# The last step of a matrix product takes its seven sub-products in an order that completes one half of the tokens first, and the outputs are multiplied by VectorE alone

## The chip, the cores and the metric

The kernel runs on one core of one Trainium2 chip. A core has TensorE (PE in the profile; PEld is its weight load), VectorE (DVE), ScalarE (ACT), GpSimd (POOL), and SyncE (SP), which here issues the transfers between the chip's memory (HBM) and the on-chip memory SBUF. TensorE writes its results into PSUM, eight banks of 128 partitions x 2 KB. The metric is the device time of one execution in microseconds (us), the median of several runs.

## The reference

One step of a hybrid flow-matching layer over 640 tokens (512 latent, 128 context), each a vector of 2048. What matters here is its end: the channel mixer's down projection, the gated residual, and the final RMSNorm, in float32.

```python
D_MODEL = 2048; D_FF = 5632; RMS_EPS = 1e-6

def _rmsnorm(x, g):
    xf = x.astype(F32)
    y = xf * lax.rsqrt(jnp.mean(xf * xf, axis=-1, keepdims=True) + RMS_EPS)
    return (y * g).astype(x.dtype)

def _layer(x, mod, s0, shift_fn, lp):
    ...
    h = _rmsnorm(x, lp['norm2_g']) * (1.0 + sc2) + sh2
    ff = (jax.nn.silu(h @ lp['w_ffn_gate']) * (h @ lp['w_ffn_up'])) @ lp['w_ffn_down']
    return x + g2 * ff, s_fin

y_prompt = _rmsnorm(x_ctx, final_norm_g)      # 128 tokens
y_sample = _rmsnorm(x_lat, final_norm_g)      # 512 tokens
```

## The kernel before

All 640 tokens stand side by side as columns (T = 640), and the model's 2048 channels as 16 blocks of 128 partitions. Only the last stage is touched by the change: `ff @ w_ffn_down`, and what follows it.

**Seven products instead of eight.** Output channels are made in pairs of blocks (m = 0, 1), tokens in two halves (h = 0: columns 0 to 319, h = 1: columns 320 to 639), the sum over D_FF in two halves. That is a 2x2 by 2x2 block product, and `seven` (L1581) computes it by seven products M1 to M7 of sums of blocks. `PORD` (L1337) is their order: 1, 2, 3, 7, 5, 6, 4. With h first, the outputs are: (0,0) = M1+M2; (1,0) = M1+M6+M5+M3; (0,1) = M1+M6+M7+M4; (1,1) = M1+M6+M7+M5. In the reference's terms two token blocks of 128 (t = 3, 4) lie wholly in h = 1, two (t = 0, 1) in h = 0, and t = 2 lies in both.

**Weights.** Each product's weight block (`rawd`, 128x512) is split by `parts` (L1388) into `hi` (ScalarE) and `lo` (VectorE, `raw - hi`), three buffers of each; each product is then 12 matmuls of 128 x 320 (L1602 to L1604). Sums of weight blocks are made by GpSimd (L1515): `t3` for M7 and the new b12 for M5 before the first product, b22 for M6 and b21 for M4 in place after the third.

**Steps.** A step is one channel pair n in one chunk of the D_FF sum; there are six chunks of eight pairs. In the last chunk n runs from 7 down to 0; each product starts from a sum kept in SBUF (`acc`), which `filled` (L1892) brings into a PSUM bank two products ahead (matmul L1898, ScalarE copy L1899). `Last` (L1831) then joins the seven results of a pair into `cs[0]`, `cs[1]`: VectorE L1851 to L1867, and `out` (L1837, L1840), which multiplies by the gate and adds the residual `xs` (loaded by `load_x1`, L1829, over the buffers of the pair before). The results come to `Last` through a queue `hooks`, three products late (`lag`). `rows` (L1872) turns a finished pair with ten TensorE transposes (L1880), copies it to `acc` as rows of tokens (L1881) and sums squares into `sse` (L1884), both on ScalarE. Through `later`, `out` for h = 1 runs in the third product and `rows` in the fifth product of the following step.

**The end.** After the last pair (n = 0): L1945 to L135 make 1/rms of all five token blocks; then ten output tiles (five token blocks x two halves of the channels, 128x1024, 512 KB each) are multiplied by 1/rms and by `final_norm_g` (which `fg` holds in `acc`), t = 0 to 4 in order. For t = 0, 2, 4 VectorE does both in one instruction (L1957). For t = 1, 3 ScalarE scales (L1954) and GpSimd multiplies (L1955). SP sends each tile (L1958).

The program is ordered per engine by a scheduler from the order of the code and from priorities; each engine then takes its own list strictly in order.

Of the kernel before, what the change touches and what calls it, by code (L numbers as in the profile page):

```python
# [19 lines left out]
P = 128  # L20
D = 2048
KB = D // P
T = 640
NT = T // P
HALF = T // 2
# [11 lines left out]
RMS_EPS = 1e-6  # L37
# [13 lines left out]
CHK = (3, 3, 4, 4, 4, 4)  # L51
# [4 lines left out]
ROWO = 4  # L56
# [31 lines left out]
def flow_step(ctx: ExitStack, tc, x_prompt, x_sample, state_rwkv, c, c_ctx, w_mod, b_mod,  # L88
              norm1_g, w_in, mu_shift, w0, w2, a0, a2, g2, k_k, k_a, r_k, gn_w, gn_b,
              gmlp_ln_g, gmlp_ln_b, w_spatial, b_spatial, w_out, norm2_g, w_ffn_gate,  # L90
              w_ffn_up, w_ffn_down, final_norm_g, y_prompt, y_sample, new_state, dbg=None):
    nc = tc.nc
# [20 lines left out]
    ident = cp.tile([P, P], F32, name="ident")  # L113
# [20 lines left out]
    def rsqrt(out, in_):  # L134
        return G.tensor_tensor(out=out, in0=in_, in1=mhalf.to_broadcast(list(in_.shape)), op=ALU.pow)  # L135
# [1199 lines left out]
    X = {}  # L1335
    t1, t2 = slice(0, HALF), slice(HALF, T)
    PORD = (1, 2, 3, 7, 5, 6, 4)  # L1337

    def xpool(i, j):
        return xep if i < 3 and j < 4 else xcp if j < 4 else xdp  # L1340
# [237 lines left out]

        return pP.tile([P, 512], F32, tag="P", name=f"P{i}")[:, 0:HALF], False

    def seven(b11, b12, b21, b22, x, hook, nk=4, bank=fresh, last=True):  # L1581
# [6 lines left out]
        src = {1: b11, 2: b21, 3: b22, 7: t3, 5: b12, 6: b22, 4: b21}  # L1588
        order = [raw for i in PORD for raw in src[i]]

        ready = [parts(order.pop(0), nk)]
        for o, i in enumerate(PORD):
            ps, filled = bank(i)
            nq = len(b11)
            for q in range(nq):
                hi, lo = ready.pop()
                if order:
                    ready.append(parts(order.pop(0), nk))
                for k in range(nk):
                    xk = x(i, 4 * q + k)  # L1600
                    f, l = q == 0 and k == 0 and not filled, q == nq - 1 and k == nk - 1 and last
                    TE.matmul(ps, hi[:, k, :], xk[:, 0, :], start=f, stop=False)  # L1602
                    TE.matmul(ps, hi[:, k, :], xk[:, 1, :], start=False, stop=False)  # L1603
                    TE.matmul(ps, lo[:, k, :], xk[:, 0, :], start=False, stop=l)  # L1604
# [190 lines left out]

    dn = ctx.enter_context(tc.tile_pool(name="dn", bufs=1))
    acc = dn.tile([P, 8, 7 * HALF], F32, name="acc")
    sse = dn.tile([P, NT, 8], F32, name="sse")
# [32 lines left out]
    class Last:  # L1831
# [11 lines left out]
        def __call__(self, o, p):  # L1843
            n, ps = self.n, self.ps
            ps[PORD[o]] = p
            if o == 1:
                self.xs = xqs.pop(n)
                self.cs = [xap.tile([P, T], F32, tag=next(ctags), name="cd") for _ in range(2)]
                self.tp = tp = xap.tile([P, 2, HALF], F32, tag="rs2", name="tp")
                S.copy(tp[:, 0], ps[1])  # L1850
                V.tensor_add(self.cs[0][:, t1], ps[2], tp[:, 0])  # L1851
                self.out(0, 0)
            elif o == 4:
                act = self.cs[1]
                S.copy(act[:, t2], ps[5])
                V.tensor_add(act[:, t1], ps[3], act[:, t2])
            elif o == 5:
                act, pa, pq = self.cs[1], self.tp[:, 0], self.tp[:, 1]
                V.tensor_add(pq, ps[6], pa)
                V.tensor_add(act[:, t1], act[:, t1], pq)  # L1860
                V.tensor_add(pq, ps[7], pq)
                V.tensor_add(act[:, t2], act[:, t2], pq)
                self.out(1, 0)
            elif o == 6:
                nc.sync.dma_start(acc[:, n, 5 * HALF:5 * HALF + 256],
                                  final_norm_g[n * 256:(n + 1) * 256].partition_broadcast(P))
                V.tensor_add(self.cs[0][:, t2], ps[4], self.tp[:, 1])  # L1867
                later.append((2, lambda: (self.out(1, 1), self.out(0, 1))))
                later.append((ROWO, self.rows))
                load_x1(n - 1)  # L1870

        def rows(self):  # L1872

            n, cs = self.n, self.cs
            for q0 in (0, 2, 4):
# [6 lines left out]
                for t in range(nt):  # L1882
                    junk = dn.tile([P, 256], F32, tag="junk", name="junk2")
                    S.activation(junk, pr[:, t], AF.Square, accum_out=sse[:, q0 + t, n:n + 1])  # L1884

    later = []
    NC = len(CHK)

    fill = [(n, i) for n in range(7, -1, -1) for i in PORD]
    banks = {}  # L1890

    def filled(n, i):  # L1892
# [10 lines left out]
    for s, (c, n) in enumerate(steps):  # L1903
# [12 lines left out]
            bank = fresh  # L1916
        if c >= NC - 2 and (final or turn):
            lag[0] = LAST_LAG
        for o in seven(b11, b12, b21, b22, lambda i, k: XD[i, k], None if turn else Last(n) if final else Sum(n),
                       CHK[c], bank, not turn):  # L1920
            if s % 8 == 6 and c < NC - 1 and o in (2, 3, 4):
                load(c + 1, (1, 2, 7)[o - 2])
            if turn:
                now(turn_ops(c + 1), o)
            elif after and o == 0:
                put_in(6)
                direct(c, 4)
            if o > 2:
                next(dloads, None)
            if final and after and o == 2:  # L1930
                load_x1(n)
            while later and o >= later[0][0]:
                later.pop(0)[1]()
            if s == len(steps) - 1 and o == 5:
                while hooks:
                    hooks.pop(0)()
    while hooks:
        hooks.pop(0)()
    for _, work in later:
# [1 line left out]
    xcx.close()  # L1941
    xex.close()
    fin = ctx.enter_context(tc.tile_pool(name="fin", bufs=5))
    rs = dn.tile([P, NT], F32, name="rse")
    V.tensor_reduce(out=rs, in_=sse, axis=AX.X, op=ALU.add)  # L1945
    V.tensor_scalar(rs, rs, 1.0 / D, RMS_EPS, op0=ALU.mult, op1=ALU.add)
    rsqrt(rs, rs)
    fg = acc[:, :, 5 * HALF:5 * HALF + 256]
    for t in range(NT):
        for h in range(2):  # L1950
            out = fin.tile([P, 4, 256], F32, tag=f"out{h}", name="out")
            src, f = (ap[:, 4 * h:4 * h + 4] for ap in (acc[:, :, t * 256:(t + 1) * 256], fg))
            if t == 1 or t == 3:
                S.activation(out, src, AF.Copy, scale=rs[:, t:t + 1])  # L1954
                G.tensor_tensor(out=out, in0=out, in1=f, op=ALU.mult)  # L1955
            else:
                V.scalar_tensor_tensor(out=out, in0=src, scalar=rs[:, t:t + 1], in1=f, op0=ALU.mult, op1=ALU.mult)  # L1957
            nc.sync.dma_start(yrows(t)[:, h * 1024:h * 1024 + 1024], out.rearrange("p n c -> p (n c)"))  # L1958
    xax.close()

# [28 lines left out]
```

## Time and profile before

| what | us |
|---|---|
| median of 3 runs | 3312.3 (3306.03 to 3312.47) |
| the profiled execution's own time | 3317.92 |
| its span, first to last instruction | 3316.1 |
| last matmul of the last step starts | 3289.72 |
| 1/rms is there, output tiles begin | 3296.05 |
| last output tile is sent | 3311.77 |

Times in the profile are microseconds from the span's start. A row of the timeline gives start, length, engine, line, operation, output <- inputs, shape, and, in brackets, how long the engine stood idle before it and what ended that. A row of the table by stretches gives from:to, the length, the busy time of PE, PEld, DVE, ACT and POOL (with counts), the granted TensorE clock, the share of the 16 DMA engines, and GB/s.

### The profile page before, as it was taken

To read this page: it belongs to the slowest core of one execution; us is meant where nothing else is said; L and a number is where in the kernel's file an instruction comes from. 1 tells how busy PE (TensorE), PEld (TensorE's weight loads), DVE (VectorE), ACT (ScalarE), POOL (GpSimd) and SP (SyncE) were. 2 spreads that over 40 slices of the span, in tenths; PEclk is the share of its full clock that TensorE was granted. 3 is DMA by queue.
4 is the path that set the end of the run, shared out by engine and by line. 5 is a ranking of instruction groups with operands and counts; after the bars stand their busy time and mean duration, and the time that the engine had idled before them with its cause. 6 is when DMAs were issued, how large, how long until landed. Compare 5 with 4: busy or idle time off the path is not lost.

```text
span 3316.1 us, 72388 instructions
## 1 busy us (share of the span) xinstructions
PE 3151.8 (95%) x28216; PEld 2912.2 (88%) x28216; DVE 2409.3 (73%) x4152; ACT 1452.3 (44%) x3163; POOL 1278.7 (39%) x1114
## 2 busy tenths in 40 slices
PE   6899999999999999998999999999999999999996
PEld 3688788778877888888999999999999999999996
DVE  4448767766866677767877777877778787877787
ACT  3334444444443444334644444444444445444365
POOL 0001122222212113333155655656656555555543
PEclk8899999999999999999999999999999999999998
DMA  8767676767667488735534343443443454553453
GB/s 318 247 180 212 184 203 186 184 182 202 187 179 217 129 273 272 237 118 158 166 103 123 118 121 118 120 128 108 125 127 103 129 185 150 162 156 116 139 162 118
DMA packets 740142, 550.88 MB, mean 166 GB/s; under 512 B 140712, under 2 KB 673208, under 8 KB 730968
## 3 DMA queue, kind: packets, MB, share of 16 engines
q1 hardware_dynamic: 727480, 532.57, 53.7%
q0 software_dynamic: 9984, 13.13, 1.7%
q8 instruction: 222, 3.64, 0.5%
q14 instruction: 120, 0.98, 0.1%
q10 hardware_dynamic: 2336, 0.57, 0.1%
HBM read 437.79 MB, written 110.95 MB: 165 GB/s over the span
## 4 chain that ended last, share of the span: by engine, by line
PE 74%; DVE 10%; DMA 6%; issue 5%; POOL 3%; ACT 2%; SPq 0%; DVEq 0%; ACTq 0%; POOLq 0%
PE P L1604 15%; PE P L1603 15%; PE P L1602 15%; PE big L188 4%; PE big L190 4%; PE big L189 4%; PE pG L636 2%; PE pm L881 2%; DMA raw<-in_w_in_dram 2%; DMA wt<-in_w_mod_dram 1%; PE big L1013 1%; DVE lo L1392 1%; PE big L1449 1%; PE big L1447 1%; PE big L1448 1%
## 5 line engine op out<-in xcount | busy, mean ns | idle before, releaser
L1602 PE MATMUL P<-xo,hi 128*128 128x320 f32 x2352 | 728.2, 310 | 3.3 <-ACT hi L1391 3.3
L1604 PE MATMUL P<-xo,lo 128*128 128x320 f32 x2352 | 728.3, 310 | 2.0 <-DVE lo L1392 1.9
L1603 PE MATMUL P<-xo,hi 128*128 128x320 f32 x2352 | 728.1, 310 | 0.0
L1392 DVE TENSOR_TENSOR lo<-raw,hi 128x512 fp32r<-128x512 f32 x532 | 513.7, 969 | 169.1 <-ACT hi L1391 164.5
L1391 ACT CAST hi<-raw 128x512 fp32r<-128x512 f32 x532 | 330.7, 622 | 496.8 <-PE P L1603 389.7
L188 PE MATMUL big<-h_hi,hi 128*128 128x320 f32 x1376 | 452.3, 329 | 8.4 <-ACT hi L166 4.9
L1602 PEld LDWEIGHTS P<-xo,hi 128*128 128x128 f32 x2352 | 442.7, 188 | 3.5 <-ACT hi L1391 3.5
L1604 PEld LDWEIGHTS P<-xo,lo 128*128 128x128 f32 x2352 | 442.6, 188 | 2.8 <-DVE lo L1392 2.8
L1603 PEld LDWEIGHTS P<-xo,hi 128*128 128x128 f32 x2352 | 442.6, 188 | 0.0
L190 PE MATMUL big<-h_hi,lo 128*128 128x320 f32 x1376 | 435.1, 317 | 1.3 <-DVE lo L167 1.3
L189 PE MATMUL big<-h_lo,hi 128*128 128x320 f32 x1376 | 435.0, 316 | 0.7 <-DVE h_lo L345 0.7
L1515 POOL TENSOR_TENSOR raw<-raw 128x512 f32<-128x512 f32 x252 | 407.7, 1627 | 14.9 <-DVE lo L1392 3.3
L1604 PE MATMUL P<-xd,lo 128*128 128x320 f32 x1232 | 383.5, 311 | 14.0 <-DVE lo L1392 13.9
L1602 PE MATMUL P<-xd,hi 128*128 128x320 f32 x1232 | 382.0, 310 | 2.7 <-ACT hi L1391 0.9
L1603 PE MATMUL P<-xd,hi 128*128 128x320 f32 x1232 | 380.6, 309 | 0.0
L167 DVE TENSOR_TENSOR lo<-raw,hi 128x512 fp32r<-128x512 f32 x268 | 187.2, 701 | 218.9 <-ACT hi L166 214.8
L188 PEld LDWEIGHTS big<-h_hi,hi 128*128 128x128 f32 x1376 | 263.7, 192 | 75.7 <-issue 48.3
L166 ACT CAST hi<-raw 128x512 fp32r<-128x512 f32 x268 | 165.9, 619 | 274.7 <-PE big L189 124.4
L1391 ACT CAST hi<-rawd 128x512 fp32r<-128x512 f32 (+1 forms) x288 | 168.9, 587 | 241.5 <-PE P L1603 196.3
L189 PEld LDWEIGHTS big<-h_lo,hi 128*128 128x128 f32 x1376 | 264.3, 192 | 7.0 <-issue 3.5
L190 PEld LDWEIGHTS big<-h_hi,lo 128*128 128x128 f32 x1376 | 263.7, 192 | 7.5 <-DVE lo L167 3.0
L1604 PEld LDWEIGHTS P<-xd,lo 128*128 128x128 f32 x1232 | 231.2, 188 | 20.4 <-DVE lo L1392 19.9
(378 smaller groups left out, 6270.0 us busy)
## 6 DMA issues: line engine op xcount, KB each, us to landing
wt<-in_w_mod_dram SPq DMA_DIRECT2D x96, 1024.0 KB
raw<-in_w_ffn_gate_dram SPq DMA_DIRECT2D x182, 256.0 KB
raw<-in_w_ffn_up_dram SPq DMA_DIRECT2D x182, 256.0 KB
rec<-d_S SPq DMA_DIRECT2D x80, 576.0 KB
raw<-in_w_in_dram SPq DMA_DIRECT2D x172, 256.0 KB
rawd<-in_w_ffn_down_dram SPq DMA_DIRECT2D x128, 256.0 KB
raw<-in_w_out_dram SPq DMA_DIRECT2D x96, 256.0 KB
xd<-d_os SPq DMA_DIRECT2D x66, 320.0 KB
```

Of the source, the lines that this page charges most:

```text
L166: S.copy(hi, raw)
L167: V.tensor_sub(lo, raw, hi.bitcast(F32))
L188: TE.matmul(halves[hf], hi[:, k, :], h_hi[:, kb, s], start=(kb == 0), stop=False)
L189: TE.matmul(halves[hf], hi[:, k, :], h_lo[:, kb, s], start=False, stop=False)
L190: TE.matmul(halves[hf], lo[:, k, :], h_hi[:, kb, s], start=False, stop=(kb == KB - 1))
L636: TE.matmul(two[h][:, cc - c0, :], XZ[:, cc, h, :, :].rearrange("p s t -> p (s t)"), R[:, cc, :, :].rearrange("p s t -> p (s t)"), start=T ...
L1391: S.copy(hi[:, 0:nk], raw[:, 0:nk])
L1392: V.tensor_sub(lo[:, 0:nk], raw[:, 0:nk], hi[:, 0:nk].bitcast(F32))
L1515: G.tensor_tensor(out=o[:, 0:nk], in0=p[:, 0:nk], in1=q[:, 0:nk], op=ALU.subtract)
L1602: TE.matmul(ps, hi[:, k, :], xk[:, 0, :], start=f, stop=False)
L1603: TE.matmul(ps, hi[:, k, :], xk[:, 1, :], start=False, stop=False)
L1604: TE.matmul(ps, lo[:, k, :], xk[:, 0, :], start=False, stop=l)
```

## The change

In the last step alone (pair n = 0 of the last chunk) the products are taken in the order `PEND` = 1, 6, 7, 5, 4, 3, 2, so that after five of them h = 1 has all it needs. For this the weight sums of M6 and M4 are made before the first product, into two new buffers (`s6`, `s4`), no longer in place after the third. A new class `End` takes each result as soon as its product is done (lag 0) and adds gate times result directly onto the residual (`put`), one instruction per product and output. After the fifth product it transposes t = 3, 4, sums their squares and makes their 1/rms; after the sixth and the seventh it does t = 0, 1, 2, one block m at a time. The pair before (n = 1) has its `out` and `rows` in the first and second product of the last step, not in the third and fifth. All ten output tiles are made without GpSimd: nine by VectorE's one instruction, one (t = 3, upper channels) by a ScalarE scale, for which `acc` was multiplied by `fg` beforehand by VectorE (L1914 of the new code). The tiles leave in the order t = 3, 4, 0, 1, 2.

```diff
+    PEND = (1, 6, 7, 5, 4, 3, 2)
...
+        s6, s4 = b22, b21
+        if end:
+            s6, s4 = ([xap.tile([P, 4, P], F32, tag=next(wtags), name="rawd")] for _ in range(2))
+            combine(s6, b22, b12)
+            combine(s4, b21, s6)
+        src = {1: b11, 2: b21, 3: b22, 7: t3, 5: b12, 6: s6, 4: s4}
+        seq = PEND if end else PORD
...
-            if i == 3:
+            if i == 3 and not end:
                 combine(b22, b22, b12)
                 combine(b21, b21, b22)
...
-                later.append((2, lambda: (self.out(1, 1), self.out(0, 1))))
-                later.append((ROWO, self.rows))
+                later.append((2 if n > 1 else 0, lambda: (self.out(1, 1), self.out(0, 1))))
+                later.append((ROWO if n > 1 else 1, self.rows))
...
+    class End(Last):
+        def put(self, m, h, src, base):
+            for (lo, hi, v) in seg(h):
+                s = slice(h * HALF + lo, h * HALF + hi)
+                V.scalar_tensor_tensor(out=self.cs[m][:, s], in0=src[:, lo:hi], scalar=modc[5][:, 2 * self.n + m, v:v + 1],
+                                       in1=base[m][:, s], op0=ALU.mult, op1=ALU.add)
+        def __call__(self, o, p):
+            n = self.n
+            if o == 0:
...
+                S.copy(self.tp[:, 0], p)
+                self.put(0, 0, p, self.xs)
+                for t in EARLY:
+                    a = acc[:, 4:8, t * 256:(t + 1) * 256]
+                    V.tensor_tensor(out=a, in0=a, in1=fg[:, 4:8], op=ALU.mult)
+            xs, cs, pa, pq = self.xs, self.cs, self.tp[:, 0], self.tp[:, 1]
+            if o == 1:
+                V.tensor_add(pq, p, pa)
+                self.put(1, 0, pq, xs)
+            elif o == 2:
+                V.tensor_add(pq, p, pq)
+                self.put(0, 1, pq, xs)
+                self.put(1, 1, pq, xs)
...
+            elif o == 3:
+                self.put(1, 1, p, cs)
+                self.put(1, 0, p, cs)
+            elif o == 4:
+                self.put(0, 1, p, cs)
+                pr = pP.tile([P, 2, 256], F32, tag="P", name="prd")
+                self.turn(pr, 0, 3, (1, 0))
+                self.turn(pr, 1, 4, (1, 0))
+                S.copy(acc[:, n, 768:1280].rearrange("p (t c) -> p t c", c=256), pr)
+                for t in range(2):
+                    self.square(pr[:, t], sse[:, 3 + t, n:n + 1])
+                scale(3, 5, 8)
+            elif o > 4:
+                m = 6 - o
+                self.put(m, 0, p, cs)
...
+                for t in range(3):
+                    self.turn(pr[t // 2], t % 2, t, (m,))
+                for t in range(3):
+                    self.square(pr[t // 2][:, t % 2, c], sse[:, t, 8 if m else n:9 if m else n + 1])
+                if not m:
+                    scale(0, 3, 9)
...
+    EARLY = (3,)
+    def scale(a, b, k):
+        r = rse[:, a:b]
+        V.tensor_reduce(out=r, in_=sse[:, a:b, 0:k], axis=AX.X, op=ALU.add)
+        V.tensor_scalar(r, r, 1.0 / D, RMS_EPS, op0=ALU.mult, op1=ALU.add)
+        rsqrt(r, r)
...
+            if end:
+                lag[0] = 0
+                while hooks:
+                    hooks.pop(0)()
...
-    for t in range(NT):
-        for h in range(2):
+    for t in (3, 4, 0, 1, 2):
+        for h in (1, 0):
...
-            if t == 1 or t == 3:
-                S.activation(out, src, AF.Copy, scale=rs[:, t:t + 1])
-                G.tensor_tensor(out=out, in0=out, in1=f, op=ALU.mult)
+            if h and t in EARLY:
+                S.activation(out, src, AF.Copy, scale=rse[:, t:t + 1])
             else:
-                V.scalar_tensor_tensor(out=out, in0=src, scalar=rs[:, t:t + 1], in1=f, op0=ALU.mult, op1=ALU.mult)
+                V.scalar_tensor_tensor(out=out, in0=src, scalar=rse[:, t:t + 1],
+                                       in1=fg[:, 4 * h:4 * h + 4], op0=ALU.mult, op1=ALU.mult)
```

GpSimd's list at its end, before. The `rawd` tiles are weight blocks; 39687 and 39660 are b22 and b21 of the pair n = 1, 39882 and 39855 those of the last step, n = 0.

```order
L1515 TENSOR_TENSOR t3_39946<-rawd_39882,rawd_39929 128x512
L1515 TENSOR_TENSOR rawd_39929<-rawd_39929,rawd_39751 128x512
L1515 TENSOR_TENSOR rawd_39687<-rawd_39687,rawd_39734 128x512
L1515 TENSOR_TENSOR rawd_39660<-rawd_39660,rawd_39687 128x512
L1515 TENSOR_TENSOR rawd_39882<-rawd_39882,rawd_39929 128x512
L1515 TENSOR_TENSOR rawd_39855<-rawd_39855,rawd_39882 128x512
L135 TENSOR_TENSOR rse_40174<-rse_40174,mhalf_82 128x5
```

The same place after; 39950 is `s6`, 39951 is `s4`, and 39688 and 39661 are now b22 and b21 of n = 1.

```order
L1516 TENSOR_TENSOR t3_39947<-rawd_39883,rawd_39930 128x512
L1516 TENSOR_TENSOR rawd_39930<-rawd_39930,rawd_39752 128x512
L1516 TENSOR_TENSOR rawd_39950<-rawd_39883,rawd_39930 128x512
L1516 TENSOR_TENSOR rawd_39951<-rawd_39856,rawd_39950 128x512
L1516 TENSOR_TENSOR rawd_39688<-rawd_39688,rawd_39735 128x512
L1516 TENSOR_TENSOR rawd_39661<-rawd_39661,rawd_39688 128x512
L135 TENSOR_TENSOR rse_33043<-rse_33043,mhalf_82 128x2
```

The last step's two sums moved ahead of the two of the pair n = 1; the four output multiplications that stood at the end of the list are gone.

VectorE's list at its end, before: joining of the last pair, 1/rms, and six output tiles.

```order
L1862 TENSOR_TENSOR cd<-cd,tp 128x320
L1867 TENSOR_TENSOR cd<-P_40099,tp 128x320
L1840 SCALAR_TENSOR_TENSOR cd<-cd,modc_90,x1d 128x192
L1840 SCALAR_TENSOR_TENSOR cd<-cd,modc_90,x1d 128x128
L1840 SCALAR_TENSOR_TENSOR cd<-cd,modc_90,x1d 128x192
L1840 SCALAR_TENSOR_TENSOR cd<-cd,modc_90,x1d 128x128
L1945 TENSOR_REDUCE rse<-sse 128x5
L1946 TENSOR_SCALAR rse<-rse 128x5
L1957 SCALAR_TENSOR_TENSOR out<-acc,rse 128x1024 x6
```

The same place after. P_40094 is the PSUM bank of the sixth product, P_40128 that of the seventh.

```order
L1901 SCALAR_TENSOR_TENSOR cd<-P_40094,modc_90,cd 128x320
L1966 TENSOR_REDUCE rse<-sse 128x2
L1967 TENSOR_SCALAR rse<-rse 128x2
L2037 SCALAR_TENSOR_TENSOR out<-acc,rse 128x1024
L1901 SCALAR_TENSOR_TENSOR cd<-P_40128,modc_90,cd 128x320
L2037 SCALAR_TENSOR_TENSOR out<-acc,rse 128x1024 x2
L1966 TENSOR_REDUCE rse<-sse 128x3
L1967 TENSOR_SCALAR rse<-rse 128x3
L2037 SCALAR_TENSOR_TENSOR out<-acc,rse 128x1024 x6
```

Three output tiles moved ahead of the second 1/rms, and one of them ahead of the last product's joining. L1914 went forward too, to the step of n = 3: VectorE has it between that step's L1864 and L1867 (L1856 and L1859 before).

More of the change, by code (lines that the diff above doesn't have):

```diff
@@ L1579, in fresh, with seven @@
         return pP.tile([P, 512], F32, tag="P", name=f"P{i}")[:, 0:HALF], False
-    def seven(b11, b12, b21, b22, x, hook, nk=4, bank=fresh, last=True):
+    def seven(b11, b12, b21, b22, x, hook, nk=4, bank=fresh, last=True, end=False):
         def combine(out, a, b):
@@ L1886, in flow_step @@
+    EARLY = (3,)
+    fg = acc[:, :, 5 * HALF:5 * HALF + 256]
+    def scale(a, b, k):
[3 more added lines that the diff above has]
+        rsqrt(r, r)
     later = []
     NC = len(CHK)
-    fill = [(n, i) for n in range(7, -1, -1) for i in PORD]
+    fill = [(n, i) for n in range(7, -1, -1) for i in (PORD if n else PEND)]
     banks = {}
@@ L1918, in flow_step @@
             lag[0] = LAST_LAG
-        for o in seven(b11, b12, b21, b22, lambda i, k: XD[i, k], None if turn else Last(n) if final else Sum(n),
-                       CHK[c], bank, not turn):
+        end = s == len(steps) - 1
+        work = None if turn else End(n) if end else Last(n) if final else Sum(n)
+        for o in seven(b11, b12, b21, b22, lambda i, k: XD[i, k], work, CHK[c], bank, not turn, end):
+            if end:
+                lag[0] = 0
+                while hooks:
+                    hooks.pop(0)()
             if s % 8 == 6 and c < NC - 1 and o in (2, 3, 4):
@@ L1933, in flow_step @@
                 later.pop(0)[1]()
-            if s == len(steps) - 1 and o == 5:
-                while hooks:
-                    hooks.pop(0)()
     while hooks:
```

31 lines of the change are left out of this document (21 added, 10 removed).

## The prediction

> **What bounds the kernel now.** The span comes first:
>
> ```profile
> span 3316.1 us, 72388 instructions
> ```
>
> The execution's own time is 3317.92 us, 1.8 us above its span and 5.6 us above the median of 3312.3; I make the sum on the span and carry the difference over to the median. Before the last stage the change leaves the work as it was, so I read the end: first the table by stretches (busy PE, PEld, DVE, ACT, POOL, then clock, DMA share, GB/s).
>
> ```profile
> 3290.00:3296.00 6.00, 1.23 (x10) 0.76 (x8) 2.11 (x8) 3.51 (x13) 1.16 (x1) 0.92 0.00 0
> 3296.00:3312.00 16.00, 0.00 (x0) 0.00 (x0) 15.69 (x6) 4.27 (x4) 12.20 (x5) 0.50 0.66 262
> ```
>
> For 6 us nothing streams out, then for 16 us VectorE is full and the DMA is not (0.66). The timeline tells why:
>
> ```profile
> 3289.72 0.31 PE L1604 MATMUL P<-xd,lo 128*128 128x320 f32 x1
> 3290.07 0.49 DVE L1867 TENSOR_TENSOR cd<-P,tp 128x320 f32<-128x320 f32 x1
> 3290.47 1.26 DVE L1840 SCALAR_TENSOR_TENSOR cd<-cd,modc,x1d 128x192 f32<-128x192 f32 x4
> 3291.53 0.87 PE L1880 MATMUL prd<-ident,cd 128*128 128x128 f32 x6 [1.17 <-DVE cd L1840]
> 3292.22 0.58 ACT L1881 COPY acc<-prd 128x512 f32<-128x512 f32 x1 [0.36 <-PE prd L1880]
> 3293.32 0.41 ACT L1884 ACTIVATE junk<-prd 128x256 f32<-128x256 f32 x1
> 3293.85 0.38 ACT L1884 ACTIVATE junk<-prd 128x256 f32<-128x256 f32 x1
> 3294.36 0.20 DVE L1945 TENSOR_REDUCE rse<-sse 128x5 f32<-128x40 f32 x1 [2.62 <-ACT junk L1884]
> 3294.84 1.17 POOL L135 TENSOR_TENSOR rse<-rse,mhalf 128x5 f32<-128x5 f32 x1 [14.37 <-DVE rse L1946]
> 3296.05 1.15 ACT L1954 ACTIVATE out<-acc,rse 128x1024 f32<-128x1024 f32 x1 [1.72 <-POOL rse L135]
> 3296.05 1.28 DVE L1957 SCALAR_TENSOR_TENSOR out<-acc,rse 128x1024 f32<-128x1024 f32 x1 [1.28 <-POOL rse L135]
> 3297.25 3.45 DVE L1957 SCALAR_TENSOR_TENSOR out<-acc,rse 128x1024 f32<-128x1024 f32 x1
> 3310.47 1.27 DVE L1957 SCALAR_TENSOR_TENSOR out<-acc,rse 128x1024 f32<-128x1024 f32 x1
> ```
>
> The chain is last matmul, join, transposes, squares, 1/rms, output tiles. The first and the last L1957 take 1.27 to 1.28 us; those between are seen with GpSimd's multiply in the groups (minimum, median, maximum in ns):
>
> ```profile
> L1957 DVE SCALAR_TENSOR_TENSOR out<-acc,rse x6: 1273/3354/3450, 3296.1 to 3310.5; 128x1024 f32<-128x1024 f32 x6
> L1955 POOL TENSOR_TENSOR out<-out,acc x4: 2347/3317/3319, 3297.3 to 3306.1; 128x1024 f32<-128x1024 f32 x4
> ```
>
> GpSimd's four run from 3297.3 to about 3309.4, beside exactly the four long ones of VectorE: the two engines take turns. The sending, by issues and stretches:
>
> ```profile
> 3297.40 0.34 SPq L1958 DMA_DIRECT2D out_dram<-out  x1
> 3311.77 0.33 SPq L1958 DMA_DIRECT2D out_dram<-out  x1
> ...
> 3298.00:3298.50 0.50, 0.00 (x0) 0.00 (x0) 0.50 (x1) 0.50 (x2) 0.50 (x1) 0.50 0.59 238
> 3302.00:3306.00 4.00, 0.00 (x0) 0.00 (x0) 4.00 (x2) 0.00 (x0) 4.00 (x2) 0.50 1.02 407
> 3314.50:3315.00 0.50, 0.00 (x0) 0.00 (x0) 0.00 (x0) 0.00 (x0) 0.00 (x0) 0.50 0.15 49
> ```
>
> With a backlog it moves 407 GB/s, so a 512 KB tile takes about 1.295 us; data begins some 0.8 us after an issue (238 of 407 in the half microsecond after 3298.00 places it at 3298.2). The last bytes move at about 3314.57 (49 of 407 in the last half microsecond), 1.53 before the span ends.
>
> **The change: the outputs.** Without GpSimd nine multiplies cost VectorE 1.20 each (3296.05 to 3297.25), less than a tile's 1.295 in the DMA. Four tiles go early, six wait for the second 1/rms. From its start: first multiply 1.20, issue and start 0.07 + 0.8 (3297.25, 3297.40 and 3298.2 give about this), then 6 x 1.295 = 7.77, together 9.85. Before, 3296.05 to 3314.57 was 18.52. Term: **-8.67**. The four early tiles are over in time: their multiplies end by 3294.3 in the order below, and their data, 5.2 us from about 3292.1, by 3297.3, ahead of 3297.8. The scaled copy that ScalarE makes of one tile (1.15) lies beside VectorE.
>
> The Trainium skill, page "SBUF — State Buffer", section "Summary: rules for kernel authors", says to estimate such a transfer by about 358 GB/s, limited by the memory outside. By it six tiles would be 6 x 1.465 = 8.79, an estimate from that page: 1.0 later, a gain smaller by that. The trace moves 407, and the measurement decides.
>
> **When the second 1/rms comes.** Three more rows from the last step, and GpSimd's power by number of elements:
>
> ```profile
> 3284.54 1.25 PE L1880 MATMUL prd<-ident,cd 128*128 128x128 f32 x10
> 3284.65 0.55 DVE L1840 SCALAR_TENSOR_TENSOR cd<-cd,modc,x1d 128x320 f32<-128x320 f32 x1 [2.10 <-DMA x1d<-d_x]
> 3288.01 0.41 PE L1602 MATMUL P<-xd,hi 128*128 128x320 f32 x1 [0.20 <-ACT P L1899]
> ...
> L135 POOL TENSOR_TENSOR ys<-ys,mhalf x16: 1957/1967/2110, 1229.4 to 1443.3; 128x10 f32<-128x10 f32 x16
> L135 POOL TENSOR_TENSOR rs<-ss,mhalf x5: 548/550/572, 10.3 to 26.3; 128x1 f32<-128x1 f32 x5
> ```
>
> The power costs 0.55, 1.17 and 1.97 for 1, 5 and 10 elements, so about 0.39 + 0.157 each: 0.71 for two, 0.86 for three. On the clock of before: the fifth product ends at 3285.8 (3284.5, and the ten transposes of the pair before now stand ahead). The join of h = 1, 0.55 (a 320 wide row, in two pieces somewhat more), is done at 3286.7, four transposes at 3287.0, a copy and two squares (0.58 + 2 x 0.53) at 3288.6, reduce and scale 0.45, power 0.71: first outputs at 3290.1. The transposes inside the sixth and seventh product push the last matmul by six x 0.125 less the 0.20 of waiting at 3288.01, so to an end of 3290.4 or a little later. VectorE is then in an output tile (3290.1 to 3291.3), and the join of the last product is queued behind it; it ends at 3291.85. Three transposes, squares and copies beside: 3292.5, then three squares at 0.53 pitch, 3294.2. On VectorE two more tiles stand ahead of the reduce, 3291.85 + 2 x 1.2 = 3294.25: even. From the last square to the outputs were 1.72 with a power of 1.17; with 0.86 it is 1.41: six multiplies begin at **3295.65**. Before 3296.05, term **-0.4**. So the shorter join and the early half give nearly nothing here: an output tile stands where the wait was.
>
> **GpSimd's two sums that moved forward.** They now stand ahead of the sums of n = 1. There the trace shows how the two engines stop each other:
>
> ```profile
> 3260.21 1.43 POOL L1515 TENSOR_TENSOR rawd<-rawd 128x512 f32<-128x512 f32 x1
> 3260.41 1.78 DVE L1392 TENSOR_TENSOR lo<-rawd,hi 128x512 fp32r<-128x512 f32 x1
> 3263.27 1.40 POOL L1515 TENSOR_TENSOR rawd<-rawd 128x512 f32<-128x512 f32 x1 [1.63 <-DVE lo L1392]
> 3263.44 1.38 DVE L1840 SCALAR_TENSOR_TENSOR cd<-cd,modc,x1d 128x128 f32<-128x128 f32 x1
> 3264.74 0.68 DVE L1392 TENSOR_TENSOR lo<-t,hi 128x512 fp32r<-128x512 f32 x1
> 3264.75 1.83 POOL L1515 TENSOR_TENSOR rawd<-rawd 128x512 f32<-128x512 f32 x1
> 3265.34 1.45 DVE L1840 SCALAR_TENSOR_TENSOR cd<-cd,modc,x1d 128x192 f32<-128x192 f32 x1
> 3267.38 1.28 DVE L1392 TENSOR_TENSOR lo<-rawd,hi 128x512 fp32r<-128x512 f32 x2
> ...
> 3266.17 0.31 PE L1604 MATMUL P<-xd,lo 128*128 128x320 f32 x1
> 3268.11 0.42 PE L1604 MATMUL P<-xd,lo 128*128 128x320 f32 x1
> ```
>
> A subtraction of VectorE that takes 0.68 alone takes 1.78 begun inside a sum of GpSimd, and ends 0.55 after it. A sum that starts beside VectorE's (3264.75) ends 1.16 after the subtraction. Before, GpSimd idles 1.63 for its b22 of n = 1; `s6` and `s4` fill this gap and run on, then b22 and b21. Stepping the two lists by this rule, `lo` of the fourth product's weights (at 3264.74 before, ready 3265.42) is ready at 3267.2, where PE needs it at 3266.17: +1.1. The next `lo` (3267.38, ready by 3268.11) comes at 3269.85, another +0.7. The sum is **+1.8**.
>
> Trainium skill, "SBUF — State Buffer", section "Who interferes with whom": a VectorE instruction with two inputs in SBUF and a GpSimd instruction that reads SBUF exclude each other, and whoever issued first keeps the port to its end. It speaks against sums put beside VectorE's work; the trace agrees (1.78 against 0.68).
>
> **Small edits.** L1914 goes to the step of n = 3, into a gap:
>
> ```profile
> 3241.35 0.49 DVE L1859 TENSOR_TENSOR tp<-P,tp 128x320 f32<-128x320 f32 x1 [0.82 <-PE P L1604]
> 3278.74 2.56 SPq L1829 DMA_DIRECT2D x1d<-d_x  x2
> ```
>
> At 1.20 for 1024 columns it overhangs the 0.82 by 0.4, of which the products ahead absorb most: bounds 0 and 0.4, taken 0.1; VectorE's changed order in n = 2 the same, 0.1. SP's load of the residual `x1d` for n = 0 moves up with the rows of n = 1 that free its buffers, from 3278.74 to about 3277.1, its second half to 3277.7. Before, the row at 3284.65 still waited for it, 3.3 to 3.6 after the second issue (at about 3281). It is now wanted by the first joins at 3282.1, so some 0.7 is left: no cost taken, bound 1.5. The two new buffers, `s6` and `s4`, take places whose last user is GpSimd itself, which holds nobody up.
>
> **The sum.** -8.67 - 0.4 + 1.8 + 0.2 = -7.05: span 3309.05, own time 3310.9, and 3312.3 - 7.0 = **3305.3** on the median.
>
> **Rivals.** *The two sums cost nothing.* If GpSimd slips into gaps and the PE waits at 3266.17 and 3268.11 stay as they are, 1.8 to 2.0 come back: gain 9.05, 3303.3. For it: the first of these `lo` had 0.75 to spare, and which engine gets in first is settled by less than that. Against: by the rows it comes 1.0 past its need.
>
> *New waits in the last step.* With no lag a result is joined at once; a late `x1d` (up to 1.5), transposes that hold PE until VectorE has joined (two places, up to 1 each), and a bank returned late add 3 to 6: gain 1 to 4, 3308.3 to 3311.3. For it: 3284.65 waited 2.10 for this load. Against: the seventh product's join is covered by an output tile already.
>
> *VectorE's long multiply is its own, not GpSimd's.* Then nine take 3.35: three early ones end at 3290.1 + 3 x 3.35 + 0.55 = 3300.7, 1/rms behind them 1.35, six more 20.1, last sent at 3322.3; its data and the end 0.9 + 1.3 + 1.5 make 3326.0, with the shift of 2.0 3328.0: 11.9 slower, 3324.2 on the median. Nine multiplies and two waits break even at about 2.0 us each. Against it stand 1.28 and 1.27 of the first and the last, when GpSimd does not multiply.
>
> **How the numbers follow.** A measurement of this kernel can tell about 0.2%, 6.6 us, from no change. The forecast has 0.58, with its own range of 3303.3 to 3307.8 (gains 4.5 to 9.0: the sums between 1 and 3, the small edits to their bounds, the early tiles late by one); its middle lies just beyond 6.6, so 0.32 of it is faster and 0.26 the same. Free sums: 0.20 (0.18 faster, 0.02 same). New waits: 0.14 (0.12 same, 0.02 slower, when a bank costs every product). The long multiply: 0.04, slower. The rest, 0.04: 0.02 same, 0.02 slower. Faster 0.50, same 0.42, slower 0.08. The range goes from 3299.0 (free sums, and the lower part of the spread of the runs, whose 3306.03 to 3312.47 is 6.4 wide) to 3311.0 (new waits).
>
> **What the changed profile would show.** All nine L2037 near 1.2 to 1.3, the DMA at over 400 GB/s from the second 1/rms to the end, six tiles after a start at 3297.6 (3295.65 + 2.0). In the step of n = 1, GpSimd's four sums back to back with VectorE's rows at 1.4 to 1.8 between, and PE idle before L1604 of the fourth and fifth product, released by `lo`, 1.8 in all. The join of the last product (L1901) starts at the end of an output tile. Wrong it would be if a multiply took over 2 us with GpSimd still, if PE waited for `x1d`'s joins, or if these PE waits were absent.

## The result, and the profile after

The changed kernel takes 3301.15 us (median of 20 runs, 3294.59 to 3310.02), the kernel before 3310.55 us (median of 20, 3301.31 to 3316.28). The ratio is 0.9978 with a 95% interval of 0.9970 to 0.9985: faster by 0.22%, or 7.3 us (5.0 to 9.9); the two medians themselves lie 9.4 apart. The profiled execution took 3299.49 us.

The two profiled spans differ by 18.7 us, far more than the ratio says. To see how much of that is the change's, I take fixed points that both programs have: the three adjacent fills of PSUM banks (L1898, now L1982) ahead of each step. They stand just before the last product of the preceding step, so "step n = 1" below means from its fills to the next ones. First those ahead of n = 1 and of the last step in the timeline before, then in the one after, with its span:

```profile
3256.77 0.60 PE L1898 MATMUL P<-xd 128*128 128x320 f32 x3
3272.69 0.60 PE L1898 MATMUL P<-xd 128*128 128x320 f32 x3
```

```profile
span 3297.4 us, 72401 instructions
...
3245.58 0.60 PE L1982 MATMUL P<-xd 128*128 128x320 f32 x3
3263.11 0.60 PE L1982 MATMUL P<-xd 128*128 128x320 f32 x3
```

The start of n = 1 is 11.19 earlier after, although the code up to there is nearly the same; over all the kernels below it lies between 3233.63 and 3256.77. Two executions of a kernel below (the outputs alone), whose code is that of before up to the output tiles, have it at 3244.43 and 3244.81, 12 earlier than the profile before. So a difference of this size comes without any change, and I don't count it for the change. From that start to the end of the span there are 59.33 us before and 51.82 after: **7.5 shorter**. I read everything below from these two fixed points. In the table by stretches (PE, PEld, DVE, ACT, POOL, clock, DMA share, GB/s) the three parts of it are, after the change:

```profile
3263.11:3285.96 22.85, 18.53 (x125) 17.12 (x123) 17.99 (x38) 16.15 (x54) 1.56 (x2) 0.95 0.27 95
3285.96:3295.84 9.88, 0.00 (x0) 0.00 (x0) 7.26 (x6) 0.00 (x0) 0.00 (x0) 0.50 0.99 391
3245.58:3263.11 17.53, 15.36 (x103) 14.44 (x102) 15.41 (x20) 10.39 (x30) 8.97 (x6) 1.00 0.22 60
```

| part | before | after | difference | forecast |
|---|---|---|---|---|
| step n = 1 (fills to fills) | 15.92 | 17.53 | +1.61 | +1.8 |
| last step, to the (second) 1/rms | 23.36 | 22.85 | -0.51 | -0.4 |
| from there to the last byte | 18.52 | 9.88 | -8.64 | -8.67 |
| last byte to the end of the span | 1.53 | 1.56 | +0.03 | 0 |
| sum | 59.33 | 51.82 | -7.51 | -7.27, and +0.2 for small edits |

The group of the output multiplies (minimum, median and maximum in ns):

```profile
L2037 DVE SCALAR_TENSOR_TENSOR out<-acc,rse x9: 1277/1280/1284, 3280.6 to 3291.9; 128x1024 f32<-128x1024 f32 x9
```

The last step and the end in the timeline:

```profile
3270.60 0.55 DVE L1901 SCALAR_TENSOR_TENSOR cd<-tp,modc,x1d 128x320 f32<-128x320 f32 x1
...
3279.83 0.70 POOL L135 TENSOR_TENSOR rse<-rse,mhalf 128x2 f32<-128x2 f32 x1 [22.81 <-DVE rse L1967]
3280.56 1.28 DVE L2037 SCALAR_TENSOR_TENSOR out<-acc,rse 128x1024 f32<-128x1024 f32 x1 [0.82 <-POOL rse L135]
3281.76 0.55 DVE L1901 SCALAR_TENSOR_TENSOR cd<-P,modc,cd 128x320 f32<-128x320 f32 x1
3282.22 2.47 DVE L2037 SCALAR_TENSOR_TENSOR out<-acc,rse 128x1024 f32<-128x1024 f32 x2
3285.07 0.86 POOL L135 TENSOR_TENSOR rse<-rse,mhalf 128x3 f32<-128x3 f32 x1 [4.54 <-DVE rse L1967]
3285.96 7.26 DVE L2037 SCALAR_TENSOR_TENSOR out<-acc,rse 128x1024 f32<-128x1024 f32 x6 [0.97 <-POOL rse L135]
```

All nine multiplies take 1.28. The first join that needs `x1d` (3270.60) shows no wait for it. The join of the last product (3281.76) stands behind an output tile, as the order said. The sending, by stretches:

```profile
3282.50:3287.00 4.50, 0.65 (x3) 0.27 (x3) 3.50 (x5) 2.01 (x10) 0.86 (x1) 0.63 1.01 401
3287.00:3288.00 1.00, 0.00 (x0) 0.00 (x0) 1.00 (x2) 0.00 (x0) 0.00 (x0) 0.50 0.76 295
3288.00:3295.50 7.50, 0.00 (x0) 0.00 (x0) 5.23 (x5) 0.00 (x0) 0.00 (x0) 0.50 1.01 401
3295.50:3296.00 0.50, 0.00 (x0) 0.00 (x0) 0.00 (x0) 0.00 (x0) 0.00 (x0) 0.50 0.73 270
```

From 3282.5 to the last byte at 3295.84 (270 of 401 in the last half microsecond) the DMA is full but for a gap of a quarter of a microsecond just before 3288 (a share of 0.76 in the microsecond from 3287), between the four early tiles and the six late ones.

In the step n = 1, first VectorE's, GpSimd's and PE's rows before, then GpSimd's, VectorE's and PE's after the change:

```profile
3258.43 0.54 DVE L1840 SCALAR_TENSOR_TENSOR cd<-cd,modc,x1d 128x320 f32<-128x320 f32 x1
...
3258.53 1.60 POOL L1515 TENSOR_TENSOR t<-rawd 128x512 f32<-128x512 f32 x1 [7.85 <-DVE tp L1861]
...
3262.24 0.42 PE L1604 MATMUL P<-xd,lo 128*128 128x320 f32 x1 [0.65 <-DVE lo L1392]
```

```profile
3247.10 1.31 POOL L1516 TENSOR_TENSOR t<-rawd 128x512 f32<-128x512 f32 x1 [7.87 <-DMA rawd<-in_w_ffn_down_dram]
3248.49 1.43 POOL L1516 TENSOR_TENSOR rawd<-rawd 128x512 f32<-128x512 f32 x1
3249.99 1.40 POOL L1516 TENSOR_TENSOR rawd<-rawd 128x512 f32<-128x512 f32 x1
...
3247.24 1.51 DVE L1848 SCALAR_TENSOR_TENSOR cd<-cd,modc,x1d 128x320 f32<-128x320 f32 x1
3248.68 1.58 DVE L1870 TENSOR_TENSOR cd<-cd,tp 128x320 f32<-128x320 f32 x1
3250.19 1.75 DVE L1393 TENSOR_TENSOR lo<-rawd,hi 128x512 fp32r<-128x512 f32 x1
...
3251.99 0.41 PE L1611 MATMUL P<-xd,lo 128*128 128x320 f32 x1 [1.60 <-DVE lo L1393]
3258.55 0.41 PE L1611 MATMUL P<-xd,lo 128*128 128x320 f32 x1 [0.44 <-DVE lo L1393]
```

After the change GpSimd's `t3` (`t<-rawd`) begins 0.14 ahead of VectorE's row at 3247.24; before it began 0.10 behind the same row. Three VectorE rows in a chain each begin inside a sum of GpSimd and end after it, at 1.51, 1.58 and 1.75. PE waits 1.60 in the second product of the step and 0.44 in the fifth; before it waited 0.65, in the second.

### The profile page after: what moved, and what is told of

Same layout as the page of the kernel before. It is cut to its first block, busy times and chain, and to the rows that moved or that the text cites. A ratio compares the mean times of both kernels' runs of the same rounds, so it can differ in the third digit from the quotient of the medians.

```text
span 3297.4 us, 72401 instructions
## 1 busy us (share of the span) xinstructions
PE 3146.3 (95%) x28216; PEld 2905.9 (88%) x28216; DVE 2402.6 (73%) x4160; ACT 1448.4 (44%) x3165; POOL 1263.3 (38%) x1111
## 4 chain that ended last, share of the span: by engine, by line
PE 72%; DVE 10%; issue 6%; DMA 5%; POOL 4%; ACT 2%; SPq 0%; DVEq 0%; POOLq 0%; ACTq 0%
PE P L1611 15%; PE P L1609 15%; PE P L1610 15%; PE big L188 4%; PE big L190 4%; PE big L189 4%; PE pG L636 2%; PE pm L881 2%; DMA wt<-in_w_mod_dram 1%; DVE lo L1393 1%; DVE mx L781 1%; DMA raw<-in_w_in_dram 1%; PE big L1450 1%; PE big L1449 1%; PE big L1448 1%
```

## The experiments

Theory: GpSimd's and VectorE's instructions on two SBUF inputs exclude each other (a VectorE output tile takes 1.28 alone and 3.35 beside GpSimd's). Taking GpSimd out of the outputs makes the DMA the bound; the early half lets it start four tiles earlier; the two weight sums that moved ahead on GpSimd cost PE about 1.6. The rivals put the whole gain on one of the two, or the longer step n = 1 on something else.

All kernels in one table. "Step n = 1" and "last step to end" are from the fills in the profile to the next fills and to the end of the span; the ratio is to the kernel before on the same chip.

| kernel | step n = 1 | last step to end | together | ratio, 95% interval |
|---|---|---|---|---|
| before | 15.92 | 43.41 | 59.33 | 1 |
| the change | 17.53 | 34.29 | 51.82 | 0.9978 (0.9970 to 0.9985) |
| the change again | 17.53 | 34.35 | 51.88 | 0.9970 (0.9958 to 0.9982) |
| outputs alone | 15.37 | 40.00 | 55.37 | 0.9979 (0.9968 to 0.9990) |
| outputs alone, again | 15.64 | 40.05 | 55.69 | 0.9984 (0.9968 to 0.9999) |
| one 1/rms | 17.68 | 38.99 | 56.67 | 0.9989 (0.9973 to 1.0004) |
| without the two sums | 15.90 | 34.33 | 50.23 | 0.9971 (0.9958 to 0.9984) |
| sums later | 15.91 | 34.33 | 50.24 | 0.9964 (0.9951 to 0.9977) |
| sums later, again | 15.85 | 34.27 | 50.12 | 0.9975 (0.9963 to 0.9987) |
| GpSimd back | 17.64 | 36.66 | 54.30 | one execution |
| copy behind squares, sums later | 15.92 | 35.05 | 50.97 | one execution |
| no early scale | 17.35 | 35.37 | 52.72 | one execution |

### The outputs alone

```diff
-            if t == 1 or t == 3:
-                S.activation(out, src, AF.Copy, scale=rs[:, t:t + 1])
-                G.tensor_tensor(out=out, in0=out, in1=f, op=ALU.mult)
-            else:
-                V.scalar_tensor_tensor(out=out, in0=src, scalar=rs[:, t:t + 1], in1=f, op0=ALU.mult, op1=ALU.mult)
+            V.scalar_tensor_tensor(out=out, in0=src, scalar=rs[:, t:t + 1], in1=f, op0=ALU.mult, op1=ALU.mult)
```

> The kernel before with one edit: all ten output tiles are VectorE's one instruction, in the old order, after one 1/rms. Measured in the profile from the start of the step n = 1 (the three adjacent fills ahead of it) to the end of the span: 59.33 us before, 51.82 after the whole change. Theory (GpSimd's multiplies held VectorE up, and without them the DMA is the bound): the six long multiplies of 3.35 become ten of 1.2 to 1.3; from 1/rms to the last byte 1.28 + 0.87 + 10 x 1.295 = 15.1 instead of 18.52, so the stretch is 55.9, 3.4 shorter, and the ratio 0.9990. Rival 1 (the whole gain is GpSimd's removal, the new order of products gives nothing): 51.8, 7.5 shorter, 0.9977. Rival 2 (the whole gain is the early half; the long multiplies are hidden in the sending): 59.3, ratio 1.000.

The span, the group of the multiplies, and from the timeline the start of the last step:

```profile
span 3299.8 us, 72382 instructions
```

```profile
L1953 DVE SCALAR_TENSOR_TENSOR out<-acc,rse x10: 1280/1281/1285, 3283.1 to 3293.9; 128x1024 f32<-128x1024 f32 x10
```

```profile
3259.80 0.60 PE L1898 MATMUL P<-xd 128*128 128x320 f32 x3
```

The multiplies are ten at 1.28 instead of six with a median of 3.35. From 3259.80 to the end are 40.00, 3.4 less than the 43.41 before, as the theory has it. So, added first, the removal of GpSimd is worth 3.4 of the 9.1 that the last step and what follows it gain in the change. The stretch as a whole came out at 55.37 instead of 55.9, because the step n = 1, with the list of before, took 15.37 in this execution. The timed ratio was 0.9979, not 0.9990, at the edge of its interval, and so was run again beside the change:

> The kernel before with all ten output tiles by VectorE, once more: its profile gave 3.4 us shorter from the last step on, its timed runs 0.9979 with an interval that ends at 0.9990. Theory (the removal of GpSimd's multiplies is worth 3.4 us, and the early half 4 more): ratio 0.9990, between before and the change. Rival (the removal alone is worth as much as the whole change, and the profile misses something ahead of the last steps): 0.9978, no difference to the change on the same chip.

> The changed kernel once more, beside the outputs alone on the same chip. Both theories: ratio to before 0.997 to 0.9985, the stretch from the start of n = 1 51.5 to 52.0, the step n = 1 17.5.

This time 0.9984 against 0.9970 for the change, with the same 40.05 and 34.35 in the profiles. The timed runs alone don't separate the two, since their intervals overlap and both ratios of the outputs alone lie 2 to 4 us below the theory's 0.9990, inside their intervals; the profile's fixed points do, twice: by 5.7 us from the last step to the end, and by 3.5 and 3.8 with the longer step n = 1 of the change counted in.

### One 1/rms

```diff
-                scale(3, 5, 8)
...
+                V.memset(sse[:, 3:5, 8:9], 0.0)
...
-                    scale(0, 3, 9)
+                    scale(0, 5, 9)
```

> The changed kernel with one 1/rms of all five blocks after the last product in place of two; no output tile goes early, the order of the products and the outputs by VectorE stay. Theory (the end is the DMA's 13 us of output from the first tile on, and the early half only lets it start earlier): the join of the last product no longer waits for an output tile, 1/rms comes 0.5 to 1.0 earlier than the second one did (22.0 to 22.4 from the end of step n = 1), but all ten tiles follow it: 1.28 + 0.87 + 12.95 + 1.56 = 16.6, so the stretch from the start of n = 1 is 56.2 to 56.6 instead of 51.82, ratio 0.9992. Rival (the early half gives nothing, the gain is in the outputs' multiplies): at most 52.5, 0.998.

```profile
3251.31 0.60 PE L1982 MATMUL P<-xd 128*128 128x320 f32 x3
...
3273.76 2.48 DVE L2037 SCALAR_TENSOR_TENSOR out<-acc,rse 128x1024 f32<-128x1024 f32 x2 [1.29 <-POOL rse L135]
```

1/rms is there 22.45 after the start of the last step, 0.4 earlier than the second one of the change, and the end is at 38.99, 4.7 later than the change. So of the 9.1, with the parts added in this order: the outputs 3.4, the new order with its shorter joins 1.0 (40.0 to 39.0), the early half 4.7. From 1/rms to the end it is 16.5 here and 11.4 in the change, 5.1 less, nearly the 5.2 that four tiles take in the DMA; the later 1/rms takes 0.4 of this back.

### The two sums left out, and the two sums later

The first of these kernels has no `s6` and `s4`; it leaves these two sums out, and M6 and M4 take the blocks b22 and b21 as they are:

```diff
-            s6, s4 = ([xap.tile([P, 4, P], F32, tag=next(wtags), name="rawd")] for _ in range(2))
-            combine(s6, b22, b12)
-            combine(s4, b21, s6)
+            pass
```

> The changed kernel without the weight sums s6 and s4 (M6 and M4 then use the blocks b22 and b21 as they are: two sums are left out, all else runs). Theory (these sums, ahead of GpSimd's sums of n = 1, hold up VectorE's rows and so PE): the step n = 1 takes 15.5 to 15.9 us instead of 17.53, its PE waits on lo fall from 2.04 to at most 0.7, and the stretch from its start to the end of the span 50.2 instead of 51.82. Rival (the longer step comes from VectorE's changed list there, or belongs to that one execution): still 17.3 to 17.6, stretch 51.8.

The second has them in buffers that come free only when the sums of n = 1 were used:

```diff
-            s6, s4 = ([xap.tile([P, 4, P], F32, tag=next(wtags), name="rawd")] for _ in range(2))
+            s6, s4 = ([xap.tile([P, 4, P], F32, tag=WT[len(steps) - 2, b], name="rawd")] for b in ("22", "21"))
...
-                raw = xap.tile([P, 4, P], F32, tag=next(wtags), name="rawd")
+                WT[s, b] = next(wtags)
+                raw = xap.tile([P, 4, P], F32, tag=WT[s, b], name="rawd")
```

> The changed kernel with s6 and s4 in the places of the weight blocks b22 and b21 of n = 1, which come free only when these are used: so GpSimd's list has them behind the sums of n = 1, and no work is left out. Theory: as without the two sums, the step n = 1 takes 15.5 to 15.9, the last step is as after the change (22.9 to the second 1/rms), the stretch from the start of n = 1 to the end is 50.2 to 50.6, and the ratio to before about 0.9974 (0.9978 less 1.4 us). Rival 1 (the longer step is not from these sums): 51.8, 0.9978. Rival 2 (late sums are not ready for the second product of the last step, or their hold on VectorE now costs there): the step n = 1 is short, but the last step over 24, the stretch 52 or more.

Sums later: the fills that bound the step n = 1, and the one wait of PE inside it.

```profile
3247.16 0.60 PE L1983 MATMUL P<-xd 128*128 128x320 f32 x3
3263.07 0.60 PE L1983 MATMUL P<-xd 128*128 128x320 f32 x3
...
3252.64 0.41 PE L1611 MATMUL P<-xd,lo 128*128 128x320 f32 x1 [0.67 <-DVE lo L1393]
```

15.90 and 15.91 instead of 17.53, and 34.33 from there in both. The longer step was the sums', 1.6 us of it, and placed later they cost nothing: the last step is as short with them as without. This kernel is 9.1 us faster than before from n = 1 on, 1.6 more than the change. Its timed runs were taken again:

> The kernel with the two sums behind those of n = 1, once more. Theory: the step n = 1 15.9, from the last step to the end 34.3, together 50.2 as in its first run, and a ratio to before 0.0004 to 0.0005 below that of the change (0.9970 to 0.9978), so 0.9965 to 0.9974. Rival (its first ratio, 0.9964, came from a gain of more than these 1.6 us): 0.9960 or less.

The profile repeats it (50.12). The ratios, 0.9964 and 0.9975, lie on both sides of the expected one; against the change's 0.9978 and 0.9970 the timed runs can't show a difference of 0.05%, so the gain over the change is shown by the profiles alone.

### GpSimd back in three tiles

```diff
+            elif t < 3 and h == 0:
+                S.activation(out, src, AF.Copy, scale=rse[:, t:t + 1])
+                G.tensor_tensor(out=out, in0=out, in1=fg[:, 0:4], op=ALU.mult)
```

> The changed kernel with GpSimd back in the late output tiles: of t = 0, 1, 2 the lower channels are scaled by ScalarE and multiplied by GpSimd, the upper ones stay with VectorE's one instruction. The stretch from the start of the step n = 1 to the end of the span is 51.82 after the change. Theory (GpSimd's multiply and VectorE's exclude each other for a whole instruction): of VectorE's three late multiplies the first takes 1.28 and the two others 3.3 to 3.5, of GpSimd's the first 2.35 and the next 3.3; the last GpSimd tile is done 10.2 after the second 1/rms, its data 2.2 later: 12.4 instead of 9.88, the stretch 54.3. Rival (they run side by side, only GpSimd's own 2.35 counts): VectorE's multiplies stay at 1.28, the last tile is done at 1.2 + 3 x 2.35 = 8.25, the stretch 52.4.

The late multiplies of VectorE and GpSimd in the timeline, and behind them PE's three waits in the step n = 1:

```profile
3291.48 1.29 DVE L2040 SCALAR_TENSOR_TENSOR out<-acc,rse 128x1024 f32<-128x1024 f32 x1 [0.97 <-POOL rse L135]
3292.68 3.45 DVE L2040 SCALAR_TENSOR_TENSOR out<-acc,rse 128x1024 f32<-128x1024 f32 x1
3296.06 3.35 DVE L2040 SCALAR_TENSOR_TENSOR out<-acc,rse 128x1024 f32<-128x1024 f32 x1
3292.70 8.91 POOL L2038 TENSOR_TENSOR out<-out,acc 128x1024 f32<-128x1024 f32 x3 [1.26 <-ACT out L2037]
...
3256.47 0.42 PE L1611 MATMUL P<-xd,lo 128*128 128x320 f32 x1 [0.66 <-DVE lo L1393]
3261.45 0.41 PE L1611 MATMUL P<-xd,lo 128*128 128x320 f32 x1 [0.89 <-DVE lo L1393]
3264.07 0.41 PE L1611 MATMUL P<-xd,lo 128*128 128x320 f32 x1 [0.46 <-DVE lo L1393]
```

With GpSimd's multiply beside it, the same instruction takes 3.45 and 3.35 instead of 1.28, and the end moves from 34.29 to 36.66 after the start of the last step: that is what GpSimd's multiply costs here, measured by itself. The waits show one thing more: this kernel has the change's lists of GpSimd and VectorE in n = 1, and its waits fell at other products than in the profile of the change (0.66, 0.89 and 0.46 instead of 1.60 and 0.44), with the same sum (2.01 and 2.04). Here the 0.66 lies in the second product, as before the change, and the 0.89 and 0.46 in the fourth and fifth; `t3` began 0.07 behind VectorE's row. In the other three executions with these lists (the change again, one 1/rms, no early scale) VectorE's row was the one held up, at 1.33 to 1.66 instead of 0.54, and the waits lie in the second and the fifth product, as in the profile of the change. The step took 17.35 to 17.68 in all five.

### What sets the end: copy behind squares, and no early scale

Two edits shift the first output and the second 1/rms apart. The first, on the kernel with the later sums:

```diff
-                S.copy(acc[:, n, 768:1280].rearrange("p (t c) -> p t c", c=256), pr)
                 for t in range(2):
                     self.square(pr[:, t], sse[:, 3 + t, n:n + 1])
                 scale(3, 5, 8)
+                S.copy(acc[:, n, 768:1280].rearrange("p (t c) -> p t c", c=256), pr)
```

> The kernel with the later sums (s6 and s4 behind those of n = 1), and ScalarE's copy of t = 3, 4 behind their squares and 1/rms instead of ahead. The first 1/rms then comes 0.5 earlier, but VectorE's list has two output tiles, no longer one, ahead of the join of the last product. Compared with the kernel with the later sums: first output 17.45 after the start of the last step, second 1/rms 22.85, end of the span 34.33. Theory (the second 1/rms sets the end: from it six tiles x 1.295; the transfers of the early tiles end just before): first output about 17.0, join of the last product and second 1/rms 0.7 to 0.8 later, end 35.0 to 35.1, with a gap in the sending. Rival (the end is the sending of ten tiles in one piece, set by the first output alone): end 33.9.

The last step began at 3261.35 here. VectorE's rows in the timeline, then the sending in the table by stretches:

```profile
3278.23 2.48 DVE L2038 SCALAR_TENSOR_TENSOR out<-acc,rse 128x1024 f32<-128x1024 f32 x2 [0.37 <-POOL rse L135]
3280.63 0.55 DVE L1902 SCALAR_TENSOR_TENSOR cd<-P,modc,cd 128x320 f32<-128x320 f32 x1
3284.97 7.26 DVE L2038 SCALAR_TENSOR_TENSOR out<-acc,rse 128x1024 f32<-128x1024 f32 x6 [0.97 <-POOL rse L135]
```

```profile
3285.50:3286.00 0.50, 0.00 (x0) 0.00 (x0) 0.50 (x1) 0.00 (x0) 0.00 (x0) 0.50 0.01 0
3286.00:3287.00 1.00, 0.00 (x0) 0.00 (x0) 1.00 (x2) 0.00 (x0) 0.00 (x0) 0.50 0.00 0
```

The first output comes 0.57 earlier (16.88 instead of 17.45), the last join 0.63 later, the second 1/rms 0.77 later (23.62), and the end 0.72 later, with 1.5 us and more in which nothing is sent. The second edit is `EARLY = ()`:

> The changed kernel without its one tile by ScalarE and without L1914 (all ten tiles by VectorE's one instruction). VectorE's list then has the reduce of the second 1/rms, one more output tile, and only then its scaling. The stretch from the start of the last step to the end is 34.29 after the change, the step n = 1 17.53. Theory (the second 1/rms sets the end; VectorE is the queue in front of it): the second 1/rms comes one tile later, 1.2, and the end with it: 35.5; the step n = 3, where L1914 stood, is no shorter than 15.5. Rival (the sending of ten tiles in one piece sets the end): the first tile goes at the same time, the end stays within 0.3, 34.3 to 34.6.

```profile
3290.54 0.18 DVE L1966 TENSOR_REDUCE rse<-sse 128x3 f32<-128x27 f32 x1
3290.63 1.28 DVE L2037 SCALAR_TENSOR_TENSOR out<-acc,rse 128x1024 f32<-128x1024 f32 x1
3291.82 0.16 DVE L1967 TENSOR_SCALAR rse<-rse 128x3 f32<-128x3 f32 x1
3292.96 7.26 DVE L2037 SCALAR_TENSOR_TENSOR out<-acc,rse 128x1024 f32<-128x1024 f32 x6 [0.97 <-POOL rse L135]
```

One output tile between reduce and scaling, and the end is 1.08 later (35.37). Without L1914 the step n = 3, where it stood, took 15.89, against 15.55 in the change with it: it cost nothing there that can be seen. Both runs say the same: the second 1/rms sets the end (from it to the end of the span are 11.4 in both, as in the change), and VectorE's list ahead of it decides when it comes. But in the change itself the early tiles end only a quarter of a microsecond ahead of the late ones, so an earlier second 1/rms alone could gain no more than that.

## Why the prediction was right

- **The outputs.** Forecast 9.85 from the second 1/rms to the last byte, measured 9.88: multiplies at 1.28 in pitch of 1.2, below the 1.295 of a tile in the DMA. The experiments split this term of 8.67 as the prediction did not: 3.4 for GpSimd's removal, measured with all ten tiles behind 1/rms, and 5.1 for the four tiles that leave early.
- **The second 1/rms.** Forecast 3295.65 on the clock of before, measured 3285.96 + 9.58 = 3295.54 (9.58 is 3272.69 - 3263.11). On the way there: first outputs forecast at 3290.1 and measured at 3290.14; the last join behind an output tile, forecast at 3291.3 and measured at 3291.34; the power 0.70 for two elements and 0.86 for three, forecast 0.71 and 0.86. One step on this path was added up a little low: the last matmul was to end at 3290.4 or a little later, its addends give 3290.6, and it ended at 3290.68. That cost nothing, since the join waits for VectorE until 3291.34. With two 1/rms the last one comes only half a microsecond earlier than before; the worth of the early half lies in the four tiles.
- **The two sums.** Forecast +1.8, measured +1.61 against the profile before (PE's bracketed waits grew by 1.39 of it, from 0.65 to 2.04); against the two executions of the outputs alone, which have the old list in n = 1, +1.9 and +2.2. The mechanism holds: left out or put later, the step is 15.9. The place does not: the stepping of the lists put the waits at the fourth and fifth product. In the profile of the change the larger one lies at the second (1.60, where 0.65 stood before) and the smaller one at the fifth (0.44): GpSimd's `t3` came 0.14 ahead of a VectorE row, which the profile before, and so the stepping, had the other way round. In the run with GpSimd back, where VectorE got in first, it lies at the fourth and fifth (0.89 and 0.46), as forecast. That the size came out although the order was another was not foreseen; the runs show that the step is 1.4 to 1.8 longer than before in either order, and not why the two sums of waits agree.
- **The small edits.** Forecast +0.2. The step n = 2 takes 15.71 (3229.87 to 3245.58) against 15.62 before (3241.15 to 3256.77), the step n = 3, which has L1914, takes 15.55 against 15.91, and steps vary by 0.3 to 0.5 with the same list, so this term can't be told from nothing. The joins don't wait for `x1d`.
- **The rivals.** Free sums: refuted by the two kernels on the sums. New waits in the last step: PE shows none before its last matmul, which starts 17.68 after the fills against 17.03 before (six transposes less one wait were forecast to cost 0.55), and the path to the second 1/rms is 0.5 shorter than before. The long multiply being VectorE's own: refuted by nine at 1.28, and by 3.4 when GpSimd is put back.
- **The sum.** Forecast 7.05 us on the span (its four terms add up to 7.07), measured 7.5 in the stretch from n = 1 on, and 7.3 (5.0 to 9.9) by the ratio. The forecast of 3305.3 was 7.0 below the median of the first three runs; 20 runs put the median of before at 3310.55, not 3312.3, and that of the change at 3301.15. The forecast stood close to the 0.2% that it took as the least that can be told from no change, and the measured 0.22% does too; its interval, 0.15 to 0.30%, leaves out zero.

What stays open is why the start of n = 1 moves by up to 23 us between executions of nearly the same code; no run here was made for that. The granted clock goes with it in the timed runs: of 23 executions of the kernel before on one chip, the shortest (3298.6) had 0.986 and the longest (3325.24) 0.977. Whether it is the cause is not shown.

## What to carry to other kernels

Where two engines hold each other up as VectorE and GpSimd do here, split elementwise work over both only if the split takes less time than one engine alone; here GpSimd's share made a VectorE instruction 2.6 times longer, ten tiles kept VectorE busy for 15.7 us when split and for 12.05 when it made them all, and making them all put it below the DMA. When a final stage streams results out, count the bytes that can leave before the last dependency: four tiles sent early were worth more (4.7) than the removal of the contention (3.4). Work that is moved ahead on a side engine must be costed at the place where it lands, and giving it a buffer that comes free later is a cheap way to put it behind more urgent work.

## What the runs showed of the hardware that was not expected

With the same lists, PE's waits came at different products in different executions: 1.60 and 0.44 in the profile of the change, 0.66, 0.89 and 0.46 in the run with GpSimd back, while their sum stayed at 2.0. In the first, GpSimd got in 0.14 us ahead of VectorE, in the second 0.07 behind it. And the outputs were sent at 401 GB/s beside VectorE's multiplies, which kept their 1.28.
